# Weight tiles of a diffusion-trunk step: high part by a casting DMA, rest by an accumulating DMA

## The chip, the cores and the metric

The kernel runs on one core of a Trainium2 chip. The metric is the device time of one execution, in microseconds. The core's engines are TensorE (PE in the profile: matrix products, with its weight loads shown apart as PEld), VectorE (DVE), ScalarE (ACT), GpSimd (POOL) and SyncE (SP, which here only issues transfers). Transfers can be issued by SP, by ACT and by GpSimd; all of them are carried by the same 16 DMA engines.

## The reference

One layer of a hybrid trunk works on 128 context tokens and 512 noisy tokens, with 1024 features. All is float32:

```
h   = rmsnorm(x, norm1_w) * (1 + sc1) + sh1          # sh, sc, g from silu(cond) @ w_ada
z   = h @ w_in                                       # 1024 x 3120
out = concat(gla(z), mlstm(z)) @ w_out               # two groups of heads, both directions
x   = x + g1 * out
h   = rmsnorm(x, norm2_w) * (1 + sc2) + sh2
x   = x + g2 * (square(relu(h @ w_ff1)) @ w_ff2)     # 1024 -> 4096 -> 1024
y   = rmsnorm(x, final_norm_w)
```

The outputs are y for both groups of tokens and the final states of the two kinds of heads for the context.

## The kernel before

All 640 tokens are processed together. To keep float32 precision in TensorE's faster format fp32r, each operand a is split into a high part (a rounded to fp32r) and a rest (a minus the high part, again fp32r), and each product is made of three matmuls: high·high, high·rest and rest·high (`three`, lines 145 to 148; in the page L146, L147 and L148 stand for them). For the activations the parts are hH and hL (or gh and gl in the MLP), for the weights wh and wl.

The weights come as 94 tiles of 128 x 1024 float32 (512 KB), in the order in which the products need them: 22 tiles of the input projection w_in, 8 of the output projection w_out (these are scaled by a column on the way, four pieces to a tile), and 64 of the MLP, 32 of w_ff1 and 32 of w_ff2, four and four in turn. One tile feeds some 7 us of TensorE in the MLP.

`fetch` (L119) brings one tile: it loads the tile from HBM into the staging tile st (two buffers), through `load` (L95, which issues on SP's queue and keeps these loads in program order); ACT copies st into wh, rounding it to fp32r (the helper's line is L83); VectorE subtracts wh from st into wl (helper `split_l`, L104, shown as L105). A wl or wh buffer is free again when TensorE's last matmul on it has ended. Up to 338 us, or so, wh and wl have three buffers each (pools whp and wlp); the MLP gets two more of each (whp2 and wlp2), so that five rotate.

`weights` (L139) hands out the next tile; before that it calls `fetch` until three tiles are ready or under way (AHEAD = 2), with a raised priority. Two tiles are fetched ahead of the first call. Each engine runs its instructions in a fixed order, which a planner writes when the program is built, from its own estimates of when each becomes ready, and from the priorities; an instruction that waits on a semaphore holds up all that is behind it on its engine or queue. Only TensorE's first stage has its order written by hand.

GpSimd's own work is small: a few splits and memsets at the start, transfers of the gate rows (sb, wr, gdr), masks in the mLSTM stage, the loads of stg (512 KB each, the conditioning weights of sh2 and g2, which VectorE turns into dot products at L964), and additions at the end (L1111, L1120). The first four half tiles of w_in go another way (st0, L274 on, split by GpSimd) and are no part of the change.

Of the kernel before, what the change touches and what calls it, by code (L numbers as in the profile page):

```python
# [11 lines left out]
F32 = mybir.dt.float32  # L12
# [3 lines left out]
AF = mybir.ActivationFunctionType  # L16
ALU = mybir.AluOpType
PSUM = bass.MemoryType.PSUM

P = 128  # L20
# [30 lines left out]
def hybrid_step(ctx: ExitStack, tc: tile.TileContext, I, O):  # L51
    nc = tc.nc
# [9 lines left out]
    stp = ctx.enter_context(tc.tile_pool(name="stp", bufs=2))  # L62
# [16 lines left out]
    def behind(late, early):  # L79
        tc.add_manual_dep(late, early.name, order, reason="issue order")  # L80

    def act(out, in_, func, **kw):
        ins = nc.scalar.activation(out, in_, func, **kw)  # L83
        if func in (AF.Exp, AF.Ln, AF.Silu, AF.Sigmoid):
            behind(ins.ins, tables["set"])
            tables["users"].append(ins.ins)
        return ins
# [7 lines left out]
    def load(out, src):  # L95
        tc.keep_in_program_order(nc.sync.dma_start(out=out, in_=src))
# [7 lines left out]
    def split_l(dst, src, hi, eng=None):  # L104
        (eng or dve).tensor_tensor(out=dst, in0=src, in1=hi.bitcast(F32), op=ALU.subtract)  # L105
# [12 lines left out]

    def fetch():  # L119
        src, scale = todo.pop(0)  # L120
        st = stp.tile([P, 1024], F32, tag="st", name="st")
        load(st, src)
        hp_, lp_ = wpools[0]
        wpools.append(wpools.pop(0))
        wh = hp_.tile([P, 1024], F32R, tag="wh", name="wh")
        wl = lp_.tile([P, 1024], F32R, tag="wl", name="wl")
        if scale is None:
            act(wh, st, AF.Copy)
            split_l(wl, st, wh)
        else:  # L130
            n = 1024 // len(scale)
            for i, g in enumerate(scale):
                s = slice(n * i, n * (i + 1))
                act(wh[:, s], st[:, s], AF.Copy, scale=g)
                stt(out=wl[:, s], in0=st[:, s], scalar=g, in1=wh[:, s].bitcast(F32),
                    op0=ALU.mult, op1=ALU.subtract)
        ready.append((wh, wl))

    def weights():  # L139
        with tc.high_priority():  # L140
            while todo and len(ready) <= AHEAD:
                fetch()
        return ready.pop(0)
# [217 lines left out]
    with tc.high_priority():  # L361
        fetch()
        fetch()
# [855 lines left out]
```

## Time and profile before

| | |
|---|---|
| median of 3 runs | 846.84 us (845.81 to 847.73) |
| span of the profiled execution, from its first to its last instruction | 844.2 us |
| TensorE busy | 814.8 us (97%), granted clock 0.988 of full speed |
| VectorE busy | 517.5 us (61%) |
| ACT busy | 380.6 us (45%) |
| GpSimd busy | 84.0 us (10%) |
| moved by DMA | 92.03 MB, 109 GB/s in the mean |

The profiled execution's own time is known by its span of 844.2 us alone; the median of the runs stands 2.6 us above it. A row of the profile names a line of the kernel, an engine, the operation, and out<-in by tile names. "x64" counts instructions; a releaser ("<-PE ff L147") is what ended the idle time before an instruction. Matmuls are pipelined, so a matmul's duration is not its share of time.

### The profile page before, as it was taken

What the parts mean: (1) busy time and instruction counts of PE and PEld (TensorE: products, weight loads), DVE (VectorE), ACT (ScalarE), POOL (GpSimd) and SP (SyncE); (2) the same over time, 40 slices, a digit from 0 to 9 for tenths busy, and PEclk for the clock granted to TensorE, in tenths of its full rate; (3) what the DMA queues carried; (4) which work ended last, traced back from release to release, by engine and by line L of the source; (5) the groups of instructions that cost most, each with busy time, mean ns of one, the idle gap of its engine ahead of it and who ended that gap; (6) DMA issues with size and microseconds to landing.
All of it is one profiled execution on the core that took longest, in us unless ns stands there. A gap on an engine that the chain in (4) does not pass through costs nothing.

```text
span 844.2 us, 15844 instructions
## 1 busy us (share of the span) xinstructions
PE 814.8 (97%) x6550; PEld 767.9 (91%) x6550; DVE 517.5 (61%) x1012; ACT 380.6 (45%) x731; POOL 84.0 (10%) x106
## 2 busy tenths in 40 slices
PE   6999999999999999999999999999999999999993
PEld 2777688999988899999999999999999999999993
DVE  4768887859565579998951443443443434435735
ACT  5555458465545485446643422413314224133152
POOL 1121000120333002002100000000000000000025
PEclk9999999999999999999999999999999999999996
DMA  9916424242251073464532222222222222222003
GB/s 346 381 47 218 134 80 150 61 118 76 63 138 38 3 271 102 150 201 140 190 102 76 72 75 76 76 74 75 76 76 73 75 75 76 76 75 75 26 1 125
DMA packets 29127, 92.03 MB, mean 109 GB/s; under 512 B 3712, under 2 KB 6656, under 8 KB 28800
## 3 DMA queue, kind: packets, MB, share of 16 engines
q1 hardware_dynamic: 22032, 72.39, 26.1%
q0 software_dynamic: 3904, 12.14, 5.1%
q10 hardware_dynamic: 3120, 6.49, 2.2%
q8 instruction: 51, 0.84, 0.4%
q14 instruction: 20, 0.16, 0.1%
HBM read 87.79 MB, written 3.19 MB: 108 GB/s over the span
## 4 chain that ended last, share of the span: by engine, by line
PE 85%; DVE 7%; ACT 3%; DMA 3%; issue 1%; POOL 0%; DVEq 0%; SPq 0%; POOLq 0%; ACTq 0%
PE ff L148 18%; PE ff L146 18%; PE ff L147 18%; DMA sta<-in_ada_dram 2%; PE pn L892 2%; PE ada L231 2%; PE pt L147 1%; PE pn L897 1%; PE pt L148 1%; PE pt L146 1%; PE ob L148 1%; PE ob L147 1%; PE ob L146 1%; PE vb L148 1%; PE vb L146 1%; PE vb L147 1%
## 5 line engine op out<-in xcount | busy, mean ns | idle before, releaser
L83 ACT ACTIVATE wh<-st 128x1024 fp32r<-128x1024 f32 (+1 forms) x90 | 93.0, 1039 | 262.2 <-PE ff L147 237.3
L148 PE MATMUL ff<-hH,wl 128*128 128x258 f32 (+1 forms) x512 | 158.8, 310 | 0.0
L146 PE MATMUL ff<-hH,wh 128*128 128x258 f32 (+1 forms) x512 | 158.7, 311 | 0.0
L147 PE MATMUL ff<-hL,wh 128*128 128x258 f32 (+1 forms) x512 | 158.7, 310 | 0.0
L148 PE MATMUL ff<-gh,wl 128*128 128x384 f32 (+1 forms) x512 | 158.1, 309 | 0.0
L146 PE MATMUL ff<-gh,wh 128*128 128x384 f32 (+1 forms) x512 | 158.1, 309 | 0.0
L147 PE MATMUL ff<-gl,wh 128*128 128x384 f32 (+1 forms) x512 | 157.8, 308 | 0.0
L105 DVE TENSOR_TENSOR wl<-st,wh 128x1024 fp32r<-128x1024 f32 x86 | 109.3, 1272 | 63.9 <-ACT wh L83 63.7
L146 PEld LDWEIGHTS ff<-gh,wh 128*128 128x128 f32 x512 | 96.7, 189 | 0.3
L147 PEld LDWEIGHTS ff<-gl,wh 128*128 128x128 f32 x512 | 96.8, 189 | 0.1
L148 PEld LDWEIGHTS ff<-gh,wl 128*128 128x128 f32 x512 | 96.7, 189 | 0.1
L147 PEld LDWEIGHTS ff<-hL,wh 128*128 128x128 f32 x512 | 96.6, 189 | 0.0
L148 PEld LDWEIGHTS ff<-hH,wl 128*128 128x128 f32 x512 | 96.5, 189 | 0.0
L146 PEld LDWEIGHTS ff<-hH,wh 128*128 128x128 f32 x512 | 96.3, 188 | 0.0
L1083 DVE TENSOR_TENSOR y<-ff,y 128x384 f32<-128x384 f32 x96 | 47.0, 489 | 70.1 <-PE ff L148 70.1
L1050 DVE TENSOR_TENSOR u<-ff,r 128x384 f32<-128x384 f32 x64 | 31.2, 490 | 69.0 <-PE ff L148 69.0
L147 PE MATMUL pt<-wl,hH 128*128 128x256 f32 x160 | 46.0, 288 | 0.1
L148 PE MATMUL pt<-wh,hL 128*128 128x256 f32 x160 | 45.6, 285 | 0.0
L146 PE MATMUL pt<-wh,hH 128*128 128x256 f32 x160 | 45.5, 286 | 0.0
L1111 POOL TENSOR_TENSOR sq<-sq,jk 128x384 f32<-128x384 f32 x6 | 6.1, 1011 | 387.8 <-ACT jk L83 387.8
L105 DVE TENSOR_TENSOR gl<-u,gh 128x640 fp32r<-128x640 f32 x32 | 26.2, 822 | 23.5 <-ACT gh L83 23.5
L964 DVE SCALAR_TENSOR_TENSOR cr<-stg,cr 128x1024 f32<-128x1024 f32 x32 | 38.9, 1216 | 0.0
(346 smaller groups left out, 1643.2 us busy)
## 6 DMA issues: line engine op xcount, KB each, us to landing
st<-in_wff_dram SPq DMA_DIRECT2D x64, 512.0 KB, 3.5
sta<-in_ada_dram SPq DMA_DIRECT2D x32, 512.0 KB, 6.5
st<-in_win_dram SPq DMA_DIRECT2D x18, 512.0 KB, 4.3
stg<-in_adag_dram POOLq DMA_DIRECT2D x16, 512.0 KB, 4.1
st<-in_wout_dram SPq DMA_DIRECT2D x8, 512.0 KB, 3.5
xT<-in_xT_dram SPq DMA_DIRECT2D x8, 320.0 KB, 5.8
sb<-gdr POOLq DMA_DIRECT2D x20, 128.0 KB, 3.4
xr<-in_xT_dram ACTq DMA_DIRECT2D x8, 320.0 KB, 5.4
```

What stands on the lines that cost most here:

```text
L83: ins = nc.scalar.activation(out, in_, func, **kw)
L105: (eng or dve).tensor_tensor(out=dst, in0=src, in1=hi.bitcast(F32), op=ALU.subtract)
L146: mm(out, lhsT=ah, rhs=bh, start=start, stop=False)
L147: mm(out, lhsT=ah, rhs=bl, start=False, stop=False)
L148: mm(out, lhsT=al, rhs=bh, start=False, stop=stop)
L231: mm(pa[32 * i:32 * i + 32, 0:n], lhsT=sc[:, 4 * rnd + i, :], rhs=sts[i // m][:, n * (i % m):n * (i % m) + n], start=(rnd == 0), stop=(rnd ...
L892: mm(o[h2], lhsT=sbs[z][:, (2 * h2 + p) * P:(2 * h2 + p + 1) * P], rhs=vb[:, c, 2 * p + h2, :], start=True, stop=(c == 0))
L897: mm(o[h2], lhsT=qw[r, z, p, (c - 1) * P:c * P], rhs=C[j][r, 2 * z + p, :], start=False, stop=True)
L964: stt(out=cr[:, 2, :], in0=st, scalar=1.0, in1=cr[:, n, :], op0=ALU.mult, op1=ALU.mult, accum_out=a)
L1050: tt(out=u[:, lo:h_], in0=ps[:, 0:h_ - lo], in1=r2[:, lo:h_], op=ALU.mult)
L1083: tt(out=y[:, ft, lo:hi], in0=ps[:, 0:hi - lo], in1=y[:, ft, lo:hi], op=ALU.add)
L1111: (nc.gpsimd if lo == 0 else dve).tensor_tensor(out=sq2[:, lo:hi], in0=sq2[:, lo:hi], in1=jk[:, lo:hi], op=ALU.add)
```

## The change

For the tiles without a scale (22 of w_in, 64 of w_ff1 and w_ff2) the staging tile and VectorE's subtraction are left out. GpSimd's queue issues a transfer from HBM into wh that casts float32 to fp32r; ACT writes wl = −wh; GpSimd's queue issues a second transfer of the same 512 KB from HBM that adds onto wl, which leaves wl = w − wh. The scaled tiles of w_out keep the old way, with st loaded by SP.

```
     def fetch():
         src, scale = todo.pop(0)
-        st = stp.tile([P, 1024], F32, tag="st", name="st")
-        load(st, src)
         hp_, lp_ = wpools[0]
         wpools.append(wpools.pop(0))
         wh = hp_.tile([P, 1024], F32R, tag="wh", name="wh")
         wl = lp_.tile([P, 1024], F32R, tag="wl", name="wl")
         if scale is None:
-            act(wh, st, AF.Copy)
-            split_l(wl, st, wh)
+            nc.gpsimd.dma_start(out=wh, in_=src)
+            act(wl, wh.bitcast(F32), AF.Copy, scale=-1.0)
+            nc.gpsimd.dma_start(out=wl, in_=src, accum_op=ALU.add)
         else:
+            st = stp.tile([P, 1024], F32, tag="st", name="st")
+            load(st, src)
             n = 1024 // len(scale)
```

## Rows read from the trace of the kernel before

**Rows 1.** The page, busy us of each engine (share of the span), instructions

```profile
PE 814.8 (97%) x6550; PEld 767.9 (91%) x6550; DVE 517.5 (61%) x1012; ACT 380.6 (45%) x731; POOL 84.0 (10%) x106
```

**Rows 2.** Busy time by stretches: stretch, length, engines, granted clock, DMA share, GB/s

```profile
0.00:42.00 42.00, 33.21 (x237) 22.10 (x238) 25.10 (x56) 22.75 (x40) 7.27 (x14) 0.96 0.95 363
42.00:84.00 42.00, 39.99 (x286) 31.71 (x286) 31.62 (x54) 24.16 (x49) 9.14 (x12) 1.00 0.42 132
84.00:127.00 43.00, 41.52 (x926) 32.03 (x925) 38.34 (x75) 21.07 (x26) 0.00 (x0) 1.00 0.34 109
...
338.00:380.00 42.00, 42.00 (x290) 42.00 (x289) 40.35 (x101) 18.92 (x34) 3.17 (x6) 1.00 0.55 175
...
464.00:506.00 42.00, 42.00 (x291) 42.00 (x290) 18.86 (x31) 15.90 (x22) 0.00 (x0) 1.00 0.24 74
...
760.00:802.00 42.00, 42.00 (x289) 42.00 (x288) 27.21 (x48) 10.37 (x14) 0.00 (x0) 1.00 0.16 51
```

**Rows 3.** The chain that ended last, in order of time: start, us, what

```profile
27.41 7.58 DMA sta<-in_ada_dram
...
35.75 1.14 DVE wl L105
...
40.93 1.23 DVE wl L105
...
94.04 1.15 DVE wl L105
...
235.55 1.44 DVE wl L105
```

**Rows 4.** Instructions on the staging tile st: ns min/median/max, first and last start

```profile
L83 ACT ACTIVATE wh<-st x90: 615/1060/1077, 17.3 to 792.1; 128x1024 fp32r<-128x1024 f32 x86, 128x512 fp32r<-128x512 f32 x4
L105 DVE TENSOR_TENSOR wl<-st,wh x86: 1208/1225/3352, 35.7 to 793.3; 128x1024 fp32r<-128x1024 f32 x86
```

**Rows 5.** Timeline in the MLP, ACT and VectorE: start, us, instruction, [idle before <-releaser]

```profile
559.11 1.06 ACT L83 ACTIVATE wh<-st 128x1024 fp32r<-128x1024 f32 x1 [5.96 <-PE ff L147]
566.13 1.06 ACT L83 ACTIVATE wh<-st 128x1024 fp32r<-128x1024 f32 x1 [5.97 <-PE ff L147]
...
560.20 1.23 DVE L105 TENSOR_TENSOR wl<-st,wh 128x1024 fp32r<-128x1024 f32 x1 [0.55 <-ACT wh L83]
```

**Rows 6.** GpSimd's loads of the tile stg, and what GpSimd waited for before them

```profile
L961 POOL DMA_DIRECT2D stg<-in_adag_dram x16: 528/530/628, 133.0 to 421.9; - x16
...
  DVE cr L964: 48.3, 9
...
DMA to landing us min/median/max: 3.7/4.1/7.0
```

**Rows 7.** Waits: who waited for whom, us in total, times, longest us

```profile
POOL sq L1111 <- ACT jk L83: 387.8, 6, 382.3
```

**Rows 8.** Transfers from 440 to 790 us: queue, packets, MB, share of 16 engines; issues

```profile
q1 hardware_dynamic: 7056, 25.69, 23.7%
...
st<-in_wff_dram SPq DMA_DIRECT2D x49, 512.0 KB, 3.5
```

**Rows 9.** ACT's timeline around the first and the last tiles of the MLP

```profile
403.74 1.04 ACT L83 ACTIVATE wh<-st 128x1024 fp32r<-128x1024 f32 x1
...
792.05 1.06 ACT L83 ACTIVATE wh<-st 128x1024 fp32r<-128x1024 f32 x1 [5.96 <-PE ff L147]
```

**Rows 10.** The MLP's matmuls on ff (first start), and VectorE's evacuations of the last product

```profile
L146 PEld LDWEIGHTS ff<-hH,wh x512: 187/188/194, 374.1 to 770.4; 128*128 128x128 f32 x171
...
801.28 0.74 DVE L1103 SCALAR_TENSOR_TENSOR xr<-ff,AB,xr 128x128 f32<-128x128 f32 x2 [0.87 <-PE ff L148]
...
811.68 0.74 DVE L1103 SCALAR_TENSOR_TENSOR xr<-ff,AB,xr 128x128 f32<-128x128 f32 x2 [1.34 <-PE ff L148]
```

**Rows 11.** ACT's timeline, two copies of weight tiles in the value projection of the mLSTM

```profile
192.53 1.08 ACT L83 ACTIVATE wh<-st 128x1024 fp32r<-128x1024 f32 x1
197.54 1.06 ACT L83 ACTIVATE wh<-st 128x1024 fp32r<-128x1024 f32 x1 [0.36 <-PE vb L148]
```

## The prediction

> **What bounds the kernel now.** I read the page's busy times first [rows 1]: TensorE is busy 814.8 of 844.2 us, VectorE 61%, and GpSimd, which gets all the new transfers, 10%. The table by stretches [rows 2] says where TensorE isn't full. From 338 to 802 us, the MLP with its 64 weight tiles and the end of the output projection, it is busy for the whole of each of the eleven stretches, of which the first, the fourth and the last are shown. Before that it lacks 8.8 us in the first 42 us, and 2.0 and 1.5 in the next two stretches. So relief of VectorE can win nothing after 338 us, and the chain that ended last says how much before: its pieces that are the VectorE split of a weight tile (L105, wl) are 1.14, 1.23, 1.15 and 1.44 us, 4.96 together [rows 3]. The 7.6 us piece ahead of them is a wait for the conditioning weights, in a stretch where the 16 DMA engines are busy 0.95 of the time [rows 2, 3].
>
> The rows of the staging tile st [rows 4] count what is touched: 86 splits by VectorE (1.225 us each), 86 of the 90 copies by ACT (1.060 us), each tile of 512 KB loaded on SP's queue. How a tile comes in now is read from ACT's timeline in the MLP [rows 5]: the copy into wh starts the moment TensorE's last use of that buffer ends (releaser PE ff L147), at 559.11 and 566.13, and so on; over the MLP it is one tile each 7.05 us (below). The load was done long before, because st is a buffer of its own. From release to both halves being ready it takes 1.06 + 1.23 = 2.3 us.
>
> **The change, part by part.** *Removed:* 86 VectorE splits, 86 × 1.225 = 105 us of VectorE. Gain: at most the 4.96 us that lie on the chain; the others are covered by TensorE. *Moved at no cost on ACT:* one pass of 128x1024 over a tile stays (copy before, negated copy after). I take its 1.06 us as before.
>
> *Moved:* 86 loads from SP to GpSimd's queue, and their place in time. Before, a load needed a free st; now it writes wh itself, so it can't be issued before TensorE releases that buffer. The cast transfer, the negation, and the accumulating transfer then stand behind the release, one after another.
>
> *Added:* 86 accumulating transfers of 512 KB, on the same queue. GpSimd issues in order: its 16 loads of stg, the same size, take 0.53 us to issue and land after 4.1 us, and many stood waiting for VectorE with nothing else getting past them [rows 6]. In the MLP it is idle for 382 us on end [rows 7], so its time is free; what counts is the order of waits.
>
> I assume that in steady state the queue alternates: cast of tile j, accumulation of tile j (waits for ACT's negation, which waits for the cast), cast of tile j+1. That is the order in which they become ready if a release comes each 7.05 us and the negation is done about 5.2 us after it. Behind the waiting accumulation stands the next cast, and for that cast, later, TensorE waits. When the queue is behind, one turn of this loop costs: the accumulation's data time *a*, during which the next cast sits behind it in the queue; the cast's own 4.1 us to landing [rows 6]; the negation, 1.06 us [rows 4]; and 0.1 us for two handovers between engines (estimate: VectorE starts 0.03 us after ACT's end in [rows 5]). Together 5.26 + *a*. As long as this is below 7.05 us everything is hidden, so the tipping point is *a* = 1.79 us.
>
> What is *a*? No accumulating transfer is in this trace. A plain load of 512 KB keeps the engines busy 23.7% of 350 us over 49 loads = 1.69 us [rows 8], or 524,288 B / (363 GB/s / 0.95) = 1.37 us when they are saturated [rows 2]. Below: as cheap as a plain load, 1.7 us, loop 6.96 us, cost nothing. Above: read the source, read the destination, write it, each as a pass of its own: 3 × 1.69 = 5.1 us, loop 10.4 us. Both ends are open. I take twice the plain load, since two streams of 512 KB are read where one was, and between the two measured rates: (2 × 1.37 + 2 × 1.69) / 2 = 3.1 us. Loop: 8.36 us, which is 1.31 us a tile more than TensorE needs.
>
> The Trainium skill, Collectives: The Full Stack, section "Why ReduceScatter is half of AllGather", says that an add in the DMA path costs no cycles of its own but needs two source reads, so a reducing transfer runs at half the rate of a copy. By it *a* would be 2 × 1.69 = 3.4 us and the sum below 929 rather than 909 us; nothing in this trace shows it.
>
> Now the lateness at the end. In the MLP five buffers rotate. The first tile whose copy only waited for a release one period apart starts at 403.74 us, the last of the 64, which is 55 tiles later, at 792.05 [rows 9]: 388.3 / 55 = 7.06 us, the period of 7.05 above within rounding. From 403.74 the last tile's second half would land at 403.74 + 55 × 8.36 + 5.26 (release to accumulation issued) + 5.5 (issue to landing: 4.1 − 1.7 + 3.1) = 874.3 us. TensorE first wants its last tile for the seventh of eight output features of the last product: the evacuation of the first is at 801.28, of the sixth at 811.68 [rows 10], so at 811.7. Late by 62.6 us. The lead of five buffers is already spent in this sum: that ninth tile lands at 414.5 us by the same terms and is wanted at 374.1 + 8 × 7.05 = 430.5 [rows 10], 16 us ahead, which a deficit of 1.31 us a tile uses up in 12 tiles.
>
> The rest I put at zero net. For: up to −5 us of VectorE pieces. Against: before 35 us, where the DMA engines are full, the first tile's accumulation adds 2.7 to 3.4 us of their time (two passes). In the middle stages three buffers rotate; a fetch there takes 5.26 + 5.5 = 10.8 us instead of 2.3, within the two tiles (14 us) that lie ready. Relu and squares queue on ACT behind a negation that waits for its cast; the cover is the two buffers of u, one tile of 7 us.
>
> Sum: the span 844.2 + 62.6 = 906.8 us. The median of the runs shown, 846.84, stands 2.6 us above the span, so 909.4: I predict 909 us.
>
> **Rivals.**
> 1. *Everything hidden, VectorE's relief counts.* It needs *a* below 1.8 us, or casts issued ahead of the older accumulation, or a cast that doesn't wait for the accumulation in front of it (sharing the engines half and half, it would land at worst one cast later: 5.26 + 1.69 = 6.95 us). For it: in the MLP the engines are busy 0.24 [rows 2], so even 1.69 + 5.1 us in 7.05 fit. Time: 846.84 − 4.96 = 841.9 if the pieces on the chain go and nothing replaces them.
> 2. *Hidden, and no difference.* As 1, but the first accumulation's 2.7 to 3.4 us on the full DMA engines or the later arrivals eat the 5 us. Time: 845 to 848.
> 3. *Hidden in the MLP, paid before it.* Twenty tiles go through three buffers. Two copies already follow 5 us apart [rows 11]; where that repeats, two tiles of lead give 10 us against 10.8, and GpSimd's other transfers, waiting for other engines, can stand between them. Three to six such tiles at 2 to 3 us: 852 to 865 us.
> 4. *Accumulation far dearer.* Three passes: loop 10.36 us, last landing 403.74 + 569.8 + 12.8 = 986.3, late by 174.6: 1021 us.
>
> The Trainium skill, DMA: Bandwidth & Descriptors, section "Queues, rings and completion order", says that within one ring an engine takes descriptors in order, while it goes round-robin between queue rows. By it a cast on the same queue does wait behind the accumulation, against the last condition of rival 1, and the time is that of my sum; no run here shows it yet.
>
> **How the numbers follow.** The loop binds in the MLP: 0.60 (with *a* from 1.8 to 5.1 us, 849 to 1021 us, of which rival 4's end above 1000 us is 0.10). Rival 1 with a visible gain: 0.17. Rival 2: 0.12. Rival 3: 0.11. About 0.2%, 1.7 us, is what a measurement of this kernel can tell from no change. So faster 0.17, same 0.12, slower 0.60 + 0.11 = 0.71. The likeliest case's own range is 870 to 1000 us. The whole range reaches down to 843, which leaves out half of rival 1 (0.08), and up to 1000 (0.10 beyond).
>
> **What would show it.** Right: between 400 and 800 us TensorE's matmuls on ff (L146, its wh and wl) wait for transfers into wl; the negations on ACT follow each other at 8 us or more, not 7.05; GpSimd's issues alternate wh, wl, wh, wl with its waits on ACT; the DMA share in the MLP rises from 0.24 to over 0.5. Wrong in size: the same picture with another period; then *a* is the period less 5.26 us. Wrong altogether: negations 7.05 us apart, TensorE at 42.00 of 42.00 us; then either two casts stand ahead of an accumulation in GpSimd's order, or *a* is under 1.8 us, which the time from an accumulation's issue to its landing tells apart. If the loss is ahead of 338 us, rival 3 holds. That ACT's negation takes much more than 1.06 us, or that the cast lands far later than 4.1 us, would break the loop's other terms.

## The result, and the profile after

The changed kernel takes 927.51 us in the median of four runs (924.69 to 929.08), against 847.1 us for the kernel before (four runs, 845.81 to 847.73). The ratio is 1.0951, 95% interval 1.0927 to 1.0975: slower by 80 us, where 62.6 were forecast. The profiled execution took 924.69 us, its span is 922.9 us, 78.7 us longer than before. The new lines shift the numbers by one: L147, L148 and L149 are the three matmuls; L126 is the casting transfer, L128 the accumulating one.

The page's busy times, beside [rows 1]:

```profile
PE 838.2 (91%) x6550; PEld 787.1 (85%) x6550; DVE 404.8 (44%) x926; ACT 379.6 (41%) x731; POOL 202.5 (22%) x278
```

VectorE has 113 us less to do (86 splits), and the kernel became slower all the same. The busy times by stretches, with the columns of [rows 2], show where:

```profile
84.00:127.00 43.00, 40.81 (x953) 29.88 (x953) 35.30 (x69) 20.61 (x24) 4.48 (x7) 1.00 0.70 200
...
380.00:422.00 42.00, 39.03 (x249) 38.50 (x248) 25.07 (x57) 25.64 (x36) 15.99 (x19) 0.96 0.93 237
422.00:464.00 42.00, 38.37 (x259) 37.79 (x258) 15.61 (x38) 17.63 (x30) 8.84 (x14) 1.00 0.66 164
464.00:506.00 42.00, 41.01 (x277) 40.80 (x276) 4.43 (x11) 14.18 (x24) 7.65 (x12) 1.00 0.56 126
...
549.00:591.00 42.00, 34.44 (x209) 33.93 (x208) 8.85 (x20) 14.81 (x21) 6.00 (x9) 0.88 0.56 126
...
760.00:802.00 42.00, 35.43 (x232) 35.23 (x233) 11.45 (x26) 15.11 (x22) 7.22 (x11) 0.92 0.56 126
```

In the MLP, where TensorE was full before, it now idles up to 7.6 us of 42, while the DMA engines are busy 0.56 of the time from 464 us on: neither is the bound. TensorE lacks 3.0 and 3.6 us in the two stretches from 380 to 464 us, 1.0 in the next, and 2.6 to 7.6 in those behind it: what lead the buffers hold at the entry is used up. The first matmul on ff starts 4.5 us later than in [rows 10]:

```profile
L147 PEld LDWEIGHTS ff<-hH,wh x512: 186/188/335, 378.6 to 842.6; 128*128 128x128 f32 x171
```

So of the 78.7 us, 4.5 arise before the MLP and 74.2 in it.

TensorE's busy time has grown by 23.4 us with the same 6550 matmuls, and its granted clock is 0.962 in the mean where it was 0.988. Behind an idle time of 5.13 us that ends at 560.50 us, for instance, the granted clock is 0.50 from 561.0 to 565.6 us, the lower of its two levels (1.2 GHz). This goes with the idling and doesn't set the pace: the loop that is read next holds no step of TensorE.

GpSimd's timeline shows the queue that sets the pace (start, us, instruction, idle before and its releaser): the entry of the MLP, one turn in its middle, and the last accumulation.

```profile
387.85 0.55 POOL L126 DMA_DIRECT2D wh<-in_wff_dram  x1 [6.27 <-PE ff L149]
...
392.10 2.38 POOL L957 TENSOR_TENSOR cr<-cr 128x1024 f32<-128x1024 f32 x1 [1.59 <-ACT cr L83]
394.43 1.75 POOL L128 DMA_DIRECT2D wl<-in_wff_dram  x2
...
414.81 0.53 POOL L962 DMA_DIRECT2D stg<-in_adag_dram  x1 [4.83 <-DVE cr L965]
415.33 0.54 POOL L126 DMA_DIRECT2D wh<-in_wff_dram  x1
...
422.23 0.86 POOL L128 DMA_DIRECT2D wl<-in_wff_dram  x1 [1.60 <-ACT wl L83]
...
565.38 0.86 POOL L128 DMA_DIRECT2D wl<-in_wff_dram  x1 [7.00 <-ACT wl L83]
565.93 0.86 POOL L126 DMA_DIRECT2D wh<-in_wff_dram  x1
574.05 0.85 POOL L128 DMA_DIRECT2D wl<-in_wff_dram  x1 [7.26 <-ACT wl L83]
574.60 0.85 POOL L126 DMA_DIRECT2D wh<-in_wff_dram  x1
...
886.28 0.87 POOL L128 DMA_DIRECT2D wl<-in_wff_dram  x1 [6.72 <-ACT wl L83]
```

And ACT's timeline over the same turn:

```profile
564.03 1.06 ACT L83 ACTIVATE wl<-wh 128x1024 fp32r<-128x1024 f32 x1 [4.91 <-DMA wh<-in_wff_dram]
564.99 1.00 ACT L83 ACTIVATE u<-u,ub 128x128 f32<-128x128 f32 x2
...
572.69 1.06 ACT L83 ACTIVATE wl<-wh 128x1024 fp32r<-128x1024 f32 x1 [5.16 <-DMA wh<-in_wff_dram]
```

Read as a loop: accumulation issued at 565.38; the next tile's cast right behind it, 0.55 us later, with no wait of its own, so its buffer had long been free; the cast has landed and the negation starts at 572.69; it ends at 573.75; 0.30 us later, at 574.05, the next accumulation goes out. Nothing in this turn waits for TensorE, so the ring goes at its own period whatever TensorE does. From the 9th accumulation of the MLP (422.23) to the 64th (886.28) it turns 55 times: 464.05 / 55 = 8.44 us, against the 7.05 us that TensorE needs for a tile. In all of these turns the cast follows the accumulation within 0.8 us. Four negations have a wait that is put down to TensorE, 22.4 us together, but their turns, 8.35 to 8.72 us, are no longer than the others (7.99 to 9.86). The waits name the two edges of the ring, and then what TensorE itself waits for (us in total, times, longest):

```profile
POOL wl L128 <- ACT wl L83: 410.6, 65, 8.1
ACT wl L83 <- DMA wh<-in_wff_dram: 312.0, 56, 8.0
DVE gl L105 <- ACT gh L83: 211.1, 28, 16.2
...
PEld ff L147 <- DVE u L1051: 28.1, 5, 7.1
...
PE ff L147 <- DVE u L1051: 26.5, 5, 6.8
```

Here the profile misleads a reader who looks at TensorE alone: only 3.0 us in each product is put down to transfers into wl, and most of the rest to VectorE's evacuations. But VectorE waits 211 us for gh, the rounded squares, and these stand on ACT behind a negation that waits for its cast. One such stretch, from the timeline of all engines:

```profile
555.62 1.06 ACT L83 ACTIVATE wl<-wh 128x1024 fp32r<-128x1024 f32 x1 [7.98 <-DMA wh<-in_wff_dram]
...
558.38 0.74 ACT L83 ACTIVATE gh<-u 128x640 fp32r<-128x640 f32 x1
559.15 0.83 DVE L105 TENSOR_TENSOR gl<-u,gh 128x640 fp32r<-128x640 f32 x1 [14.54 <-ACT gh L83]
559.89 0.88 DVE L1051 TENSOR_TENSOR u<-ff,r 128x384 f32<-128x384 f32 x2
560.50 0.58 PE L147 MATMUL ff<-hH,wh 128*128 128x258 f32 x1 [5.13 <-DVE u L1051]
```

The late tile and the late evacuation have one cause, and the late evacuation ends last.

What the accumulation costs follows from the DMA engines' time between 440 and 880 us (queue, packets, MB, share of 16 engines; then the issues, KB each, median us to landing):

```profile
q0 software_dynamic: 14992, 54.60, 55.6%
...
wh<-in_wff_dram POOLq DMA_DIRECT2D x53, 512.0 KB, 6.3
wl<-in_wff_dram POOLq DMA_DIRECT2D x52, 512.0 KB, 5.6
```

Together 0.556 × 440 = 244.6 us. If a cast costs what a load does, 1.69 us [rows 8], an accumulation costs (244.6 − 53 × 1.69) / 52 = 2.98 us, 1.76 times a load. (The experiment with a plain second load, below, confirms the 1.69: the pair of cast and load keeps the engines busy 0.48 of 7.05 us, 1.69 each. Where GpSimd's queue carries accumulations alone, in the experiment with the accumulation in the MLP only, an accumulation measures 3.25 us, 1.92 times a load.)

### The profile page after: what moved, and what is told of

It is laid out like the page before. It is cut to its first block, busy times and chain, and to the rows that moved or that the text cites. A ratio compares the mean times of both kernels' runs of the same rounds, so it can differ in the third digit from the quotient of the medians.

```text
span 922.9 us, 15856 instructions
## 1 busy us (share of the span) xinstructions
PE 838.2 (91%) x6550; PEld 787.1 (85%) x6550; DVE 404.8 (44%) x926; ACT 379.6 (41%) x731; POOL 202.5 (22%) x278
## 4 chain that ended last, share of the span: by engine, by line
issue 40%; PE 32%; DMA 9%; POOL 8%; DVE 6%; ACT 5%; ACTq 0%; DVEq 0%; POOLq 0%
POOL wh L126 5%; POOL wl L128 3%; DMA sta<-in_ada_dram 3%; DMA wh<-in_wff_dram 2%; PE ada L232 2%; DMA wl<-in_wff_dram 2%; PE pt L148 2%; PE pt L149 1%; PE pn L893 1%; PE pt L147 1%; DMA stg<-in_adag_dram 1%; PE pn L898 1%; DVE cr L965 1%; PE vb L149 1%; PE vb L147 1%
## 5 line engine op out<-in xcount | busy, mean ns | idle before, releaser
L83 ACT ACTIVATE wl<-wh 128x1024 fp32r<-128x1024 f32 x86 | 91.1, 1060 | 358.7 <-DMA wh<-in_wff_dram 312.0
L147 PE MATMUL ff<-hH,wh 128*128 128x384 f32 (+1 forms) x512 | 165.1, 323 | 26.6 <-DVE u L1051 26.5
L147 PE MATMUL ff<-gh,wh 128*128 128x384 f32 (+1 forms) x512 | 161.9, 316 | 21.1 <-DVE y L1084 16.6
L149 PE MATMUL ff<-hH,wl 128*128 128x258 f32 (+1 forms) x512 | 163.3, 320 | 3.0 <-DMA wl<-in_wff_dram 3.0
L148 PE MATMUL ff<-hL,wh 128*128 128x384 f32 (+1 forms) x512 | 163.7, 320 | 0.0
L149 PE MATMUL ff<-gh,wl 128*128 128x384 f32 (+1 forms) x512 | 160.9, 314 | 3.0 <-DMA wl<-in_wff_dram 3.0
L148 PE MATMUL ff<-gl,wh 128*128 128x384 f32 (+1 forms) x512 | 160.6, 314 | 0.0
L128 POOL DMA_DIRECT2D wl<-in_wff_dram x64 | 55.4, 869 | 389.8 <-ACT wl L83 340.0
L147 PEld LDWEIGHTS ff<-hH,wh 128*128 128x128 f32 x512 | 101.9, 199 | 28.4 <-DVE u L1051 28.1
L147 PEld LDWEIGHTS ff<-gh,wh 128*128 128x128 f32 x512 | 98.8, 193 | 23.2 <-DVE y L1084 17.8
L149 PEld LDWEIGHTS ff<-hH,wl 128*128 128x128 f32 x512 | 101.6, 199 | 3.2 <-DMA wl<-in_wff_dram 3.2
L148 PEld LDWEIGHTS ff<-hL,wh 128*128 128x128 f32 x512 | 102.0, 199 | 0.0
L149 PEld LDWEIGHTS ff<-gh,wl 128*128 128x128 f32 x512 | 98.7, 193 | 3.5 <-DMA wl<-in_wff_dram 3.3
L148 PEld LDWEIGHTS ff<-gl,wh 128*128 128x128 f32 x512 | 98.9, 193 | 0.1
L126 POOL DMA_DIRECT2D wh<-in_wff_dram x64 | 51.7, 808 | 17.1 <-PE woc L149 8.5
L149 PE MATMUL pt<-wh,hL 128*128 128x256 f32 x160 | 45.8, 286 | 0.0
L148 PE MATMUL pt<-wl,hH 128*128 128x256 f32 x160 | 45.5, 285 | 0.0
L147 PE MATMUL pt<-wh,hH 128*128 128x256 f32 x160 | 45.5, 284 | 0.0
```

The source lines that it names most:

```text
L126: nc.gpsimd.dma_start(out=wh, in_=src)
L128: nc.gpsimd.dma_start(out=wl, in_=src, accum_op=ALU.add)
L147: mm(out, lhsT=ah, rhs=bh, start=start, stop=False)
L148: mm(out, lhsT=ah, rhs=bl, start=False, stop=False)
L149: mm(out, lhsT=al, rhs=bh, start=False, stop=stop)
```

## The experiments

The theory: the in-order queue makes a ring of accumulation, cast and negation, and its turn is longer than TensorE's period. Rivals: the DMA engines or the accumulating transfer as such are too slow; the loss is made before the MLP; casts into the working buffers come too late. Each ratio is to the kernel before on the same chip.

**The next cast ahead of the accumulation.** All transfers stay; only the order on GpSimd's queue changes, in the MLP (`behind` puts its first instruction after its second).

```
+    def finish(cast):
+        wh, wl, src = raw.pop(0)
+        act(wl, wh.bitcast(F32), AF.Copy, scale=-1.0)
+        a = nc.gpsimd.dma_start(out=wl, in_=src, accum_op=ALU.add)
+        behind(a.ins, cast.ins)
+        ready.append((wh, wl))
...
-            nc.gpsimd.dma_start(out=wh, in_=src)
-            act(wl, wh.bitcast(F32), AF.Copy, scale=-1.0)
-            nc.gpsimd.dma_start(out=wl, in_=src, accum_op=ALU.add)
+            c = nc.gpsimd.dma_start(out=wh, in_=src)
+            raw.append((wh, wl, src))
+            while len(raw) > (1 if 0 < len(todo) < 64 else 0):
+                finish(c)
```

> The changed kernel, with one edit: in the MLP the cast of tile j+1 stands ahead of the accumulation of tile j in GpSimd's order. If the loss is the order (a loop of cast, negation and accumulation that turns once per tile), two tiles are now under way at once, the negations come 7.05 us apart again, TensorE is full from 400 to 800 us and the time is 846 to 853 us (the changed kernel enters the MLP 4.5 us later than the kernel before, and that stays). If the accumulating transfers load the DMA engines too much (56% of them in the MLP now), or a lead of five buffers is too short for a fetch of 11 us, the period stays at 8.5 us and the time above 915 us.

Measured 859.38 us, ratio 1.0147 (1.0121 to 1.0172): 68 of the 80 us are back. Its stretches:

```profile
84.00:127.00 43.00, 38.31 (x848) 26.60 (x846) 31.75 (x63) 19.43 (x23) 3.93 (x6) 0.96 0.64 186
...
380.00:422.00 42.00, 37.35 (x233) 36.29 (x233) 22.57 (x56) 23.61 (x34) 16.22 (x21) 0.96 0.91 223
...
549.00:591.00 42.00, 42.00 (x288) 42.00 (x288) 12.34 (x25) 13.18 (x17) 8.31 (x13) 1.00 0.74 151
```

and its GpSimd timeline, in which L134 is the cast and L123 the accumulation:

```profile
562.14 0.55 POOL L134 DMA_DIRECT2D wh<-in_wff_dram  x1 [5.66 <-PE ff L159]
562.67 0.91 POOL L123 DMA_DIRECT2D wl<-in_wff_dram  x1
569.17 0.55 POOL L134 DMA_DIRECT2D wh<-in_wff_dram  x1 [5.59 <-PE ff L159]
569.71 0.90 POOL L123 DMA_DIRECT2D wl<-in_wff_dram  x1
```

The wait of the queue has changed sides: now the cast waits for TensorE's release, and the period is 7.03 us. TensorE is full with the same transfers and a higher DMA share, 0.74: the DMA engines were not the bound, the order was. The size was missed: 846 to 853 was expected, and of the 12.8 us that are left most is lost in 84 to 127 us (3.2 more than in [rows 2]) and 380 to 422 us (4.65, none before). The first of these isn't the edit's: up to 125 us the order on VectorE, ACT, GpSimd and SP is that of the changed kernel, which lacks only 0.7 us more than [rows 2] there. The profiled execution, 861.99 us, is the longest of the four (856.90 to 861.99). The two halves tried apart, below, cost 3.5 us (this order, in the MLP only) and 3.4 us (the change for w_in only); the 5.9 us between their sum and 12.8 stay unexplained.

**A plain second load.** `accum_op` is left out, so wl holds the weight itself.

> The changed kernel with the second transfer a plain casting load instead of an accumulating one, so that wl holds the weight and not the rest; everything else is in place, the wait for the negation too. It measures what the accumulation costs beyond a load. By the loop, the turn is 8.54 us now, of which the cast's wait behind the accumulation is about 2.5 us; with 1.7 us there, the turn is 7.7 us, 0.65 us a tile above TensorE's 7.05, and the time about 875 us (865 to 890). If the turn is made of fixed latencies and waits, and the kind of transfer doesn't matter, the period stays at 8.5 us and the time at 927 us. If the accumulation is nearly all of it, 850 us.

Measured 854.57 us, 1.0091 (1.0063 to 1.0119): a miss, well below the 865 to 890 expected. A turn in its GpSimd timeline:

```profile
567.43 0.53 POOL L128 DMA_DIRECT2D wl<-in_wff_dram  x1 [5.99 <-ACT wl L83]
567.95 0.54 POOL L126 DMA_DIRECT2D wh<-in_wff_dram  x1
574.02 0.53 POOL L128 DMA_DIRECT2D wl<-in_wff_dram  x1 [5.53 <-ACT wl L83]
574.97 0.53 POOL L126 DMA_DIRECT2D wh<-in_wff_dram  x1 [0.43 <-PE ff L149]
```

With a load in the accumulation's place the ring turns in 574.02 − 567.43 = 6.59 us and then waits for TensorE. From a cast's issue to the negation it is 4.71 us here (567.95 to 572.66 on ACT) and 6.76 us behind an accumulation (565.93 to 572.69): in these two turns the accumulation costs the ring 2.05 us more than a load, and that carries it from below to above 7.05 us. From 440 us on the means of 52 casts each, from issue to negation, are 4.84 and 6.48 us, which makes 1.64 us. My expectation had put the load's turn above 7.05 too.

**The cast alone** (the kernel before, with the cast in place of ACT's copy; st and VectorE's split stay):

```
-            act(wh, st, AF.Copy)
+            nc.gpsimd.dma_start(out=wh, in_=src)
             split_l(wl, st, wh)
```

> The kernel before with only the high part's casting transfer: GpSimd's queue casts into wh, the staging tile is loaded by SP and VectorE subtracts as before. No wait for another engine stands on GpSimd's queue between two casts, so the loop theory expects TensorE full in the MLP and 845 to 852 us. If the cast itself, 6.3 us to landing in the changed kernel, were what can't keep up, the time would stay above 900 us.

Measured 853.72 us, 1.0091 (1.0061 to 1.012), just above what was expected. TensorE is full from 422 us on, 42.00 of 42.00; it loses between 84 and 169 us (37.97 of 43, 37.23 of 42). The casts into the working buffers cost some 7 us in the early stages, all told, and nothing in the MLP.

**The accumulation alone** (the kernel before, but wl made by ACT's negation and the accumulating transfer):

```
             act(wh, st, AF.Copy)
-            split_l(wl, st, wh)
+            act(wl, wh.bitcast(F32), AF.Copy, scale=-1.0)
+            nc.gpsimd.dma_start(out=wl, in_=src, accum_op=ALU.add)
```

> The kernel before with only the rest's accumulation: SP loads the staging tile, ACT copies it into wh and writes the negative into wl, GpSimd's queue accumulates; VectorE does no split. On that queue stand accumulations alone, one each 7.05 us against 5.6 us to landing, so the loop theory expects TensorE full in the MLP and 846 to 853 us, with 86 us more on ACT hidden. If accumulating transfers alone were too slow, or too heavy for the DMA engines, the time would be above 900 us.

Measured 862.54, 871.23, 879.93 and 881.69 us, too far apart for a ratio: a miss. The stretches of the run of 871.23 us:

```profile
84.00:127.00 43.00, 32.58 (x655) 22.96 (x654) 27.91 (x56) 19.83 (x24) 1.73 (x2) 0.84 0.54 148
127.00:169.00 42.00, 37.17 (x558) 30.06 (x559) 24.14 (x38) 23.54 (x42) 3.94 (x5) 0.76 0.41 110
...
549.00:591.00 42.00, 42.00 (x290) 42.00 (x289) 11.56 (x25) 21.36 (x28) 5.16 (x6) 1.00 0.70 150
```

From 506 us on the MLP is as expected; between 422 and 506 us TensorE lacks 1.9 us. Most of the loss is early, where TensorE now waits for the conditioning weights; the waits between 84 and 169 us:

```profile
PEld ada L232 <- DMA sta<-in_ada_dram: 14.5, 6, 4.8
PE ada L232 <- DMA sta<-in_ada_dram: 13.3, 5, 4.6
```

Before, these two waits were 1.7 and 1.5 us. The loads stand on SP's queue, which from 42 to 169 us waited 48.4 us for ACT's copies out of st, four times and 22.0 us at the longest: the same kind of jam, on another queue. The changed kernel loads no st for these tiles, so this loss isn't its own; as a test of the accumulation's price the run says something of the MLP only.

**The change for the 22 tiles of w_in only.**

```
-        if scale is None:
+        if scale is None and len(todo) >= 64:
...
+        elif scale is None:
+            st = stp.tile([P, 1024], F32, tag="st", name="st")
+            load(st, src)
+            act(wh, st, AF.Copy)
+            split_l(wl, st, wh)
```

> The change for the 22 tiles of the input projection alone; the 64 tiles of the MLP come in as before. The theory puts nearly all of the loss into the MLP, so the time is that of the kernel before plus what the early stages lose, by the start of the MLP 4.5 us (378.6 against 374.1): 849 to 853 us. If VectorE's relief wins in the early stages, 842 to 846 us. If three buffers were the place of the loss, above 860 us.

Measured 849.92 us, 1.0043 (1.0026 to 1.006), as expected. The stages before the MLP cost 3.4 us of the 80 when the change is made there alone.

**Every second tile of the MLP plain** (half of the rests are therefore the weight itself):

```
-            nc.gpsimd.dma_start(out=wl, in_=src, accum_op=ALU.add)
+            nc.gpsimd.dma_start(out=wl, in_=src, **({} if len(todo) % 2 and len(todo) < 64 else {"accum_op": ALU.add}))
```

> The changed kernel, with every second tile of the MLP loaded a second time by a plain casting transfer instead of an accumulating one (its wl then holds the weight, not the rest). Turns of the loop on GpSimd's queue were 8.44 us in the mean with accumulations and would be 6.6 us with plain loads (6.07 from cast to second load, 0.53 to issue it), so the mean turn is 7.5 us, 0.47 us a tile above TensorE's 7.05. If turns add up along the queue, 53 of them give 25 us, and with the 7 us that the changed kernel loses elsewhere the time is 870 to 885 us. If only the slowest tile counted, or the lead of the buffers soaked up every second tile, 850 to 858 us.

Measured 883.07 us, 1.0428 (1.0409 to 1.0448), as expected. The issues of the second halves, from GpSimd's timeline:

```profile
562.40 0.53 POOL L128 DMA_DIRECT2D wl<-in_wff_dram  x1 [7.32 <-ACT wl L83]
...
569.19 0.87 POOL L128 DMA_DIRECT2D wl<-in_wff_dram  x1 [5.72 <-ACT wl L83]
...
577.26 0.53 POOL L128 DMA_DIRECT2D wl<-in_wff_dram  x1 [6.64 <-ACT wl L83]
...
583.90 0.87 POOL L128 DMA_DIRECT2D wl<-in_wff_dram  x1 [5.58 <-ACT wl L83]
```

A plain load is issued in 0.53 us, an accumulation in 0.87, which tells them apart. The turn behind a load is 6.79 and 6.64 us, behind an accumulation 8.07. Over the MLP 28 turns behind a load take 6.85 us in the mean and 27 behind an accumulation 8.46, which is the changed kernel's own turn of 8.44 but for 0.02: the ring's period follows what stands in it, tile by tile. From the 9th second half (424.18) to the 64th (844.40) the mean turn is 7.64 us, 0.59 above TensorE's period: 55 × 0.59 = 32 of the 36 us lost here.

**The loads of stg moved to SP's queue** (all sixteen). The turn was as forecast but the loss larger, which leaves the question why the ring starts late.

```
-        nc.gpsimd.dma_start(out=st, in_=I["adag"][0 if g == SH2 else 1, ft])
+        nc.sync.dma_start(out=st, in_=I["adag"][0 if g == SH2 else 1, ft])
```

> The changed kernel with the 16 loads of stg issued on SP's queue, so that GpSimd's holds nothing but weight transfers at the entry of the MLP. There the ninth accumulation was issued at 422.2 us where the forecast had 409. If the stg loads, each waiting for VectorE between the casts, made this lateness, the ninth is issued some 10 us earlier and the time is 913 to 920 us. If the DMA engines, busy 0.93 of the time from 380 to 422 us, or the order of casts set it, the time stays at 924 to 929 us.

Measured 948.97 us, 1.1222 (1.1177 to 1.1267): slower still. It is no clean test, because on SP six of these loads stood ahead of the third load of w_out, for which ACT and behind it TensorE then waited: from 338 to 380 us TensorE is busy 25.42 of 42 us, and the MLP starts 20.9 us later. From there to the end it takes 548.0 us, against 544.3.

**Only the last eight of them (those of g2) on SP:**

```
+        (nc.sync if g == G2 else nc.gpsimd).dma_start(out=st, in_=I["adag"][0 if g == SH2 else 1, ft])
```

> The changed kernel with only the eight stg loads of the MLP's first group on SP's queue, which is empty by then; the eight before it stay on GpSimd's, so that w_out's loads on SP are not held up as in the run before. If the stg loads among the casts made the ninth accumulation late (422.2 us), it is issued up to 10 us earlier, the MLP still starts at about 379 us, and the time is 915 to 922 us. If the lateness at the entry comes from the casts' own waits, 924 to 929 us.

Measured 928.14 us, 1.0975 (1.0943 to 1.1006): no gain. The MLP starts in time, but its 9th accumulation is as late as in the changed kernel, and now behind ACT's relu instead of a load of stg:

```profile
424.32 0.84 POOL L128 DMA_DIRECT2D wl<-in_wff_dram  x1 [9.11 <-ACT u L83]
```

In the changed kernel the ninth cast stands behind a load of stg that waited 4.83 us for VectorE (414.81 above). Without g2's loads it stands at 414.34 instead of 415.33, behind the eighth accumulation, which waited for its own negation until 413.79. So the theory that these loads make the entry late has fallen.

**The cast ahead, the change in the MLP only** (the first experiment's edit, and the way of before for w_in).

> The change for the 64 tiles of the MLP alone, with the cast of the next tile ahead of each accumulation; the input projection's tiles come in as in the kernel before. The early stages then lose nothing and the loop is gone, so what is left is the entry of the MLP, where TensorE lacked 4.7 us with this order: 848 to 853 us. If the 12.5 us that this order lost with the change everywhere came from the MLP itself, 857 us or more.

Measured 850.46 us, 1.0043 (1.003 to 1.0057), as expected. TensorE is at 42.00 of 42.00 from 464 us on; between 338 and 464 it lacks 4.2 us (1.93, 0.35 and 1.88 in three stretches).

**The accumulation alone, in the MLP only** (ACT's copy from st stays there, and `split_l` for w_in):

```
             act(wh, st, AF.Copy)
-            split_l(wl, st, wh)
+            if len(todo) >= 64:
+                split_l(wl, st, wh)
+            else:
+                act(wl, wh.bitcast(F32), AF.Copy, scale=-1.0)
+                nc.gpsimd.dma_start(out=wl, in_=src, accum_op=ALU.add)
```

> The kernel before with the accumulation for the 64 tiles of the MLP alone: there SP loads the staging tile, ACT copies it and writes the negative, GpSimd's queue accumulates. The variant with it everywhere lost 29 us, and its trace showed TensorE full from 506 to 802 us and short before 295. If accumulating transfers are harmless where no cast stands behind them, 846 to 851 us. If they cost in the MLP all the same, 860 us or more.

Measured 845.33 us, 0.9989 (0.9974 to 1.0004), just below what was expected, and no difference from the kernel before. 64 accumulations go through the MLP on GpSimd's queue, TensorE is at 42.00 of 42.00 us in each stretch from 338 to 800 us, and that with the DMA engines busy 0.95 from 380 to 422. An accumulation without a cast behind it costs nothing. The DMA engines' time on GpSimd's queue, which carries 50 accumulations and nothing else from 440 to 790 us:

```profile
q0 software_dynamic: 7200, 26.22, 46.4%
```

That is 0.464 × 350 / 50 = 3.25 us for one.

**Both: the cast ahead in the MLP, and g2's loads of stg on SP.**

> The change for the MLP's tiles alone, the next cast ahead of each accumulation, and the eight stg loads of the first group on SP's queue. It was 850.5 us with those loads on GpSimd's queue. If the 3.5 us left over come from that queue at the entry, 845 to 848 us, no better than the kernel before, since TensorE is full there already. If they come from the casts waiting for three buffers while the output projection runs, it stays at 849 to 852 us.

Measured 853.12 us, 1.0088 (1.0072 to 1.0104): above both ranges, no gain, but 2.7 us more than without moving the loads. Why it is more was not tried. No version beat the kernel before beyond its interval; TensorE is full in the MLP there, and nothing that relieves VectorE in it can win.

## Why the prediction was nearly right

*The sign and the place: right.* The loss is the ring on GpSimd's queue, in the MLP. Putting one cast ahead takes 68 of the 80 us away and leaves every transfer in; the change in w_in alone costs 3.4 us, so rival 3 (paid before the MLP) holds a small part only. Rivals 1 and 2 needed a turn below 7.05 us, or casts ahead of the older accumulation; the plain load shows the first condition (6.59 us, full TensorE), the cast ahead the second. Rival 4 had 10.36 us for a turn; it is 8.44.

*The turn: 8.36 us forecast, 8.44 measured.* Its terms: accumulation's data time and the cast's landing, 3.1 + 4.1 = 7.2 us forecast, 7.31 in the turn shown and 8.44 − 1.06 − 0.30 = 7.08 in the mean; negation 1.06, as forecast; handovers 0.30 from the negation's end to the accumulation alone, where 0.1 was put for both. The accumulation's 2.98 to 3.25 us lies around the 3.1 between the bounds of 1.7 and 5.1. That was a lucky guess in part: no row before spoke for twice a load against the bounds, and the loop was anything from 6.96 to 10.4 us. The run with every second tile plain splits the turn otherwise, by a little: behind a load 6.85 us, where 5.26 + 1.69 = 6.95 were forecast, and 1.61 more behind an accumulation, where 3.1 − 1.69 = 1.41 were. The rule of the Trainium skill, Collectives: The Full Stack, section "Why ReduceScatter is half of AllGather", would make it 2.0 times a load; here it is 1.76 times in the changed kernel and 1.92 times where it has the queue to itself. By the terms of the sum that rule gives 926 us and not the 929 written there. Either is nearer to the result only because another term was missing:

*The mis-sized term: "the rest I put at zero net".* The last accumulation goes out at 886.28 us; the sum had 403.74 + 55 × 8.36 + 5.26 = 868.8. Of the 17.5 us between, 464.05 − 459.8 = 4.25 are the turn's (55 × 8.36 = 459.8). The other 13.2 are there at the ninth tile: its accumulation is issued at 422.23, not 403.74 + 5.26 = 409.0. They divide so: the MLP starts 4.5 us later; the ninth cast goes out another 7.1 us later, since 415.33 − 403.74 = 11.6; and the accumulation follows it by 6.90 us, not 5.26, 1.6 us more. From the last accumulation to the end it takes 36.6 us, where the sum had 906.8 − 868.8 = 38.0, and the median stands 4.6 us above the profiled span instead of 2.6: 17.5 − 1.4 + 2.0 = 18.1 us, the whole of 927.5 − 909.4. The prediction looked at the entry only to show that 16 us of lead were there and would be used up; it took for granted that the queue begins its alternation on time. At the entry the queue holds a burst of casts into the new buffers, accumulations behind their negations, two additions of cr and eight loads of stg, while the DMA engines are busy 0.93 of the time. Which of them sets the delay stays open: without the stg loads of g2 the ninth accumulation is as late, and the additions and the burst were not tried one by one. The delay counts only because the ring can't make it up: with the plain second load the ninth tile is issued hardly earlier, at 419.58, and the kernel ends 73 us earlier.

*TensorE's own wait: half right.* I said that the matmuls would wait for transfers into wl. They do, for 3.0 us in each of the two products; most of the idle time is put down to the evacuations, through ACT's order. The prediction named that queue (relu and squares behind a waiting negation) and called it covered by two buffers of u; that holds only while the ring is in time.

*What would show it* came out as written: GpSimd alternating and waiting for ACT, negations 8.4 us apart in the mean, a DMA share of 0.56 instead of 0.24. That the cast lands 4.1 us after its issue holds in the stages before (4.3); in the MLP it is 6.3, where it goes behind the accumulation, and this part was counted as *a*.

## What to carry to other kernels

When two transfers of one tile with an engine's step between them share an in-order queue with the next tile's, they make a ring: add up its turn (data time of the second, landing of the first, the step, the handovers) and compare it with the period of the engine that bounds the stage. If it is longer, free buffers don't help (the casts here waited for none), and idle DMA engines don't either; issuing the next tile's first transfer ahead of this tile's second one breaks the ring at no cost in transfers (68 of 80 us here). Count separately how late the ring starts: at the entry of a stage the queue still holds other work.

## What the runs showed of the hardware

- An accumulating transfer of 512 KB from HBM onto fp32r data in SBUF keeps the 16 DMA engines busy for 2.98 us in the changed kernel and 3.25 where GpSimd's queue carries no other transfer, a plain or a casting one for 1.69. GpSimd's issue is 0.86 us for the accumulation and 0.53 to 0.55 for the others, though the cast that stands right behind an accumulation, 0.55 us after it, shows 0.86 too.
- Casting float32 to fp32r on the way costs nothing that these runs show: 1.69 us of engine time, landing after 4.3 us where a plain load of the same size takes 4.1 [rows 6].
- Two transfers that follow each other on GpSimd's queue are not free of each other even at a DMA share of 0.56: a cast 0.55 us behind an accumulation lands after 6.3 us instead of 4.3.
- An accumulation makes a turn of the ring 1.61 us longer than a load does (8.46 against 6.85 us in the run with every second tile plain). That is near the difference in engine time, 2.98 − 1.69 = 1.29 to 3.25 − 1.69 = 1.56 us.
- Behind 5.13 us without work TensorE was granted 0.50 of its full clock, from 561.0 to 565.6 us; in the kernel before, without idle time there, the granted clock is 1.00 in each stretch from 380 to 802 us.
